# Gate matmuls of a hybrid decoder layer: two heads stacked over 128 rows, or one head on each half of the array

## The chip, the core and the metric

The kernel runs on one core of a Trainium2 chip. The metric is the device time of one execution in microseconds; the time before is the median of 3 runs. TensorE appears in the profile as PE (matmuls) and PEld (weight loads), VectorE as DVE, ScalarE as ACT, GpSimd as POOL, SyncE (which issues most of the DMAs) as SP.

## The reference, cut to what matters

A sequence of 2048 positions with 1024 features is normalised, projected to six groups of 1024 columns, mixed by a short gated convolution (group A) and by a gated linear recurrence (group B, "LRU"), normalised head by head, gated, and projected back. The change touches only the two gates of the LRU, r and i. There are 16 heads of 64 channels; each head has its own 64 by 64 map for r and another for i:

```python
u = causal_depthwise_conv(x_in, conv_w) + conv_b
uh = u.reshape(bsz, s, N_LRU_HEADS, LRU_HEAD_DIM)          # 16 heads of 64
r = jax.nn.sigmoid(jnp.einsum('bshd,hde->bshe', uh, w_a).reshape(bsz, s, d) + b_a)
i = jax.nn.sigmoid(jnp.einsum('bshd,hde->bshe', uh, w_i).reshape(bsz, s, d) + b_i)
a = jnp.exp(RG_LRU_C * r * jax.nn.log_sigmoid(lam))
drive = jnp.sqrt(1 - a * a) * (i * u)                       # h_t = a_t h_{t-1} + drive_t
```

## The kernel before, in words

All large products run on TensorE in the type fp32r. To keep float32 accuracy each operand is split into a high part (a cast to fp32r, on ACT) and a low part (operand minus high part, on DVE or POOL), and a product is made of three matmuls: high by high, high by low, low by high. The products of the big projections are further saved by a seven-product (Strassen-like) scheme on 2 by 2 blocks: `steps` lists 48 + 16 block steps, each of seven products into PSUM banks of 128 by 512 (`mm`, line 886, twelve matmuls for a product: four blocks of the contraction by three parts).

The order of the work is written out by hand. PE goes through the steps; each step has 7 or 8 slots, a slot is one product of 12 matmuls. At each slot's start `tick()` releases what was put into the list `due` by `at(slots, f)`: the elementwise work on ACT, DVE and POOL, and a few extra matmuls. Every engine executes its instructions strictly in the order in which the slots emit them; only semaphores join the engines. Since the releases stand ahead of the slot's product, extra matmuls on PE stand between two products.

Each third step of the first 48 is an LRU step (`lru`, called for h = 0, 1 (halves of the sequence) and k = 0 to 7 (tiles of 128 channels, two heads each)): 16 LRU steps in all. After its column block has come out of PSUM, the following stands at fixed slots: the convolution u (slots 1 to 3); `sth`, the high part of u (slot 5, line 651, ACT); `stl`, the low part (slot 6, through `tt`, line 160, DVE); `gates(0)` at slot 8 and `gates(1)` at slot 10 (line 666, PE), one for each half of the 1024 positions; `sigs(0)` at slot 9 and `sigs(1)` at slot 11 (line 673, four sigmoids of 64 by 512 each, ACT); then the recurrence.

A head has 64 channels, so its map would fill only 64 of the array's 128 rows. Before, the kernel fills the other 64 with the low part. For head j the tile st[j] (128 by 1024) holds the high part of the head's u on one half of the partitions and the low part on the other, and the weights of the head are stored twice, one copy on each half of the partitions. So one matmul over 128 rows gives weight by (high + low); two matmuls, with the weights' high part `bh` and low part `bl`, give the head's r and i for 512 positions. `gates(i)` is 2 heads by 2 matmuls. Each head has its own PSUM tile ("gate" in the profile) from the pool `pss`, which has two buffers; so `gates(1)` can write head j's tile only once `sigs(0)` has read it.

The price of the layout is that high and low parts are made over 64 partitions at a time: `sth` is two casts of 64 by 1024 and `stl` two subtractions of 64 by 1024. `load_gate_w` (lines 608 to 618) fetches the doubled weights by a DMA on SP (line 612) and splits them on POOL (lines 615 and 616) into `bh` and `bl` of 128 by 256.

Other matmuls that lie between products are the head norms' sums (`head_sums`, line 559): four matmuls with weights of 128 by 64. The copies out of a product's PSUM bank are `q` (line 1220), `u` (line 1223), `rr` (line 1226) and `combine` (line 729) on ACT; they share ACT's order with the gates' sigmoids.

Of the kernel before, what the change touches and what calls it, by code (L numbers as in the profile page):

```python
# [12 lines left out]
F32 = mybir.dt.float32  # L13
F32R = mybir.dt.float32r
AF = mybir.ActivationFunctionType
ALU = mybir.AluOpType

P = 128
D = 1024
S = 2048  # L20
C = 512
NC = S // C
NB = C // P
KT = D // P
# [14 lines left out]
def hymba_kernel(ctx: ExitStack, tc: tile.TileContext, x, xt, w_in, par, lamc, w_gate, w_out, final_g, out):  # L39
    nc = tc.nc  # L40
# [6 lines left out]
    small = ctx.enter_context(tc.tile_pool(name="small", bufs=1))  # L47
    psu = ctx.enter_context(tc.tile_pool(name="psu", bufs=5, space=bass.MemoryType.PSUM))
    pss = ctx.enter_context(tc.tile_pool(name="pss", bufs=2, space=bass.MemoryType.PSUM))
# [12 lines left out]
    def wt(tag, name, n=2 * C, dt=F32, bufs=1):  # L62
        return work.tile([P, n], dt, tag=tag, bufs=bufs, name=name)
# [6 lines left out]
    def aux(name):  # L70
        return small.tile([P, C], F32, tag="aux", bufs=4, name=name)
# [69 lines left out]
    def at(slots, *fs):  # L141
        if slots == 0:
            for f in fs:
                f()
        else:
            due.append([slots, fs])
# [12 lines left out]
    def tt(out, a, b, op, eng=None):  # L159
        (eng or nc.vector).tensor_tensor(out=out, in0=a, in1=b, op=op)  # L160
# [176 lines left out]
    def hl_tile(name, n=1):  # L337
        hlc[0] += n
        return [wt("hl", name, dt=F32R, bufs=HL) for _ in range(n)]

    def hl_done(n):
        hlc[0] -= n
# [223 lines left out]
    def finish(d0, h, kt, y, sil, gain, col, row):  # L566
        v = {}

        def f1():
            nc.vector.scalar_tensor_tensor(out=sil, in0=y, scalar=gain, in1=sil,  # L570
                                           op0=ALU.mult, op1=ALU.mult)

        def store():
            for i in range(2):
                nc.sync.dma_start(yd[2 * h + i][:, :, kt, :].rearrange("b p t -> p b t"),
                                  sil[:, i * C:(i + 1) * C].rearrange("p (b t) -> p b t", b=NB))

        def f2():
            nc.scalar.activation(out=y, in_=y, func=AF.Square)
            v["qh"], = hl_tile("qh")  # L580
            nc.scalar.copy(v["qh"], y)

        def f3():
            v["ql"], = hl_tile("ql")
            tt(v["ql"], y, v["qh"].bitcast(F32), ALU.subtract)

        at(d0, f1)
        at(d0 + (1 if kt == KT and h == 0 else 2), store)
        at(d0 + 2, f2)
        at(d0 + 3, f3)  # L590
        at(d0 + 6, lambda: head_sums(h, v["qh"], v["ql"], col, row))
        at(d0 + 7, lambda: hl_done(2))

    def silu(g, late=0):
        sg = [None]

        def f1():
            sg[0] = wt("ig", "sg", bufs=IG)
            nc.scalar.activation(out=sg[0], in_=g, func=AF.Sigmoid)  # L599

        at(2 + late, f1)
        at(4 + late, lambda: tt(g, g, sg[0], ALU.mult, nc.gpsimd))
# [3 lines left out]


    def load_gate_w(k):
        bd = aux("bd")[:, 0:2 * P].rearrange("p (h m) -> p h m", h=2)
        bh = small.tile([P, 2, P], F32R, tag="bh", name="bh")  # L610
        bl = small.tile([P, 2, P], F32R, tag="bl", name="bl")
        nc.sync.dma_start(bd, w_gate[k])

        def part():
            nc.gpsimd.tensor_scalar(out=bh, in0=bd, scalar1=1.0, scalar2=0.0, op0=ALU.mult, op1=ALU.add)
            nc.gpsimd.tensor_tensor(out=bl, in0=bd, in1=bh.bitcast(F32), op=ALU.subtract)

        at(3, part)
        return bh, bl

    LO, HI = slice(0, 64), slice(64, P)
    N2 = 2 * C

    def lru(h, k, late=0):
        o1 = wt("o1", "xl", n=N2 + 4)
        g = wt("o2", "gl", bufs=O2)
        if h == 0:
            nc.gpsimd.memset(o1[:, 0:4], 0.0)
        else:
            nc.scalar.copy(o1[:, 0:4], hx[:, k, :])  # L630
        v = {}
        lw = [pt[:, LW + 8 * j + k:LW + 8 * j + k + 1] for j in range(4)]

        def c0():
            v["u"] = wt("u", "u")
            nc.scalar.activation(out=v["u"], in_=o1[:, 1:1 + N2], func=AF.Identity, scale=lw[0],  # L636
                                 bias=pt[:, LB + k:LB + k + 1])

        def cj(j):
            nc.vector.scalar_tensor_tensor(out=v["u"], in0=o1[:, 1 + j:1 + j + N2], scalar=lw[j],  # L640
                                           in1=v["u"], op0=ALU.mult, op1=ALU.add)

        def keep():
            if h == 0:
                nc.scalar.copy(hx[:, k, :], o1[:, N2:N2 + 4])

        def sth():
            v["st"] = st = hl_tile("st", 2)
            at(6, lambda: hl_done(2))
            for j, hi in enumerate((LO, HI)):  # L650
                nc.scalar.copy(st[j][hi], v["u"][hi])

        def stl():
            st = v["st"]
            for j, (hi, lo) in enumerate(((LO, HI), (HI, LO))):
                tt(st[j][lo], v["u"][hi], st[j][hi].bitcast(F32), ALU.subtract)

        def gates(i):
            sl = slice(i * C, (i + 1) * C)
            if i == 0:  # L660
                v["r"], v["i"] = wt("r", "r"), wt("ig", "i", bufs=IG)
            v["ps"] = ps = []
            for j in range(2):
                ps.append(pss.tile([P, C], F32, tag="s", name="gate"))
                for n in range(2):
                    nc.tensor.matmul(ps[j], v["gw"][n][:, j, :], v["st"][j][:, sl],  # L666
                                     start=(n == 0), stop=(n == 1))

        def sigs(i):
            sl = slice(i * C, (i + 1) * C)  # L670
            for j, (hi, lo) in enumerate(((LO, HI), (HI, LO))):
                for g_, src, bias in ((v["r"], hi, BA), (v["i"], lo, BI)):
                    nc.scalar.activation(out=g_[hi, sl], in_=v["ps"][j][src], func=AF.Sigmoid,  # L673
                                         bias=pt[src, bias + k:bias + k + 1])


        def s0():
            tt(v["u"], v["i"], v["u"], ALU.mult)

        def s1():  # L680
            v["T"] = wt("ig", "T", bufs=IG)
            nc.scalar.activation(out=v["T"], in_=v["r"], func=AF.Tanh, scale=nklam[:, k:k + 1])

        def s1b():
            nc.scalar.activation(out=v["r"], in_=v["r"], func=AF.Exp, scale=klam[:, k:k + 1])

        def s2():
            nc.scalar.activation(out=v["T"], in_=v["T"], func=AF.Sqrt)

        def s3():  # L690
            nc.vector.scalar_tensor_tensor(out=v["u"], in0=v["r"], scalar=1.0, in1=v["u"],
                                           op0=ALU.add, op1=ALU.mult)

        def s4():
            tt(v["u"], v["T"], v["u"], ALU.mult)

        def s5():
            r = v["r"]
            init = 0.0 if h == 0 else hl[:, k:k + 1]
            nc.vector.tensor_tensor_scan(out=r, data0=r, data1=v["u"], initial=init,  # L700
                                         op0=ALU.mult, op1=ALU.add)
            if h == 0:
                nc.vector.tensor_copy(hl[:, k:k + 1], r[:, N2 - 1:N2])

        def out_():
            finish(0, h, KT + k, v["r"], g, pt[:, LG + k:LG + k + 1], 2 * R, KT + k)

        def gw():
            v["gw"] = load_gate_w(k)

        def put(which, bank, other):
            dst = {11: o1[:, 4:4 + C], 12: o1[:, 4 + C:4 + N2], 21: g[:, 0:C], 22: g[:, C:N2]}[which]
            combine(dst, bank, other)
            if which == 12:
                at(1, c0)
                at(2, lambda: cj(1), lambda: cj(2), keep, gw)
                at(3, lambda: cj(3))
                for slots, *fs in ((5, sth), (6, stl), (8, lambda: gates(0)), (9, lambda: sigs(0)),
                                   (10, lambda: gates(1)), (11, lambda: sigs(1)), (12, s1, s0),
                                   (13, s1b), (14, s2, s3), (15, s4), (16, s5), (17, out_)):  # L720
                    at(slots + late, *fs)
            if which == 21:
                silu(g, late)

        return put

    def combine(dst, bank, other):
        if other is None:
            nc.scalar.copy(dst, bank)
        else:  # L730
            tt(dst, bank, other, ALU.add)
# [188 lines left out]
    with tc.manual_schedule(engines={ENG.PE, ENG.Activation, ENG.DVE, ENG.Pool, ENG.SP}):  # L920
# [176 lines left out]
        for n in range(PLAIN, N):  # L1097
            kind, h, k = steps[n]
# [185 lines left out]
```

## Time and profile before

| | |
|---|---|
| time, median of 3 runs | 1418.91 us (1418.45 to 1420.51) |
| profiled execution, first to last instruction | 1418.1 us, 0.8 us under that median |
| mean granted TensorE clock | 0.981 |
| PE busy | 1336.5 us, 5732 matmuls |
| DVE busy | 1069.9 us |
| ACT busy | 782.6 us |
| POOL busy | 242.6 us |

A row of the timeline gives the start in us, the length, the engine, the line, the operation, output<-inputs, the shape, the count, and in brackets the idle time of the engine before it with what ended it. A matmul's length runs from its issue to its modelled end, so consecutive matmuls overlap: what a matmul costs the stream is the distance from its start to the next one's start. A row of the groups gives the count, then busy us and mean ns of one, then the engine's idle time before them.

### The profile page before, as it was taken

To read this page: it belongs to the slowest core of one execution; us is meant where nothing else is said; L and a number is where in the kernel's file an instruction comes from. 1 tells how busy PE (TensorE), PEld (TensorE's weight loads), DVE (VectorE), ACT (ScalarE), POOL (GpSimd) and SP (SyncE) were. 2 spreads that over 40 slices of the span, in tenths; PEclk is the share of its full clock that TensorE was granted. 3 is DMA by queue.
4 is the path that set the end of the run, shared out by engine and by line. 5 is a ranking of instruction groups with operands and counts; after the bars stand their busy time and mean duration, and the time that the engine had idled before them with its cause. 6 is when DMAs were issued, how large, how long until landed. Compare 5 with 4: busy or idle time off the path is not lost.

```text
span 1418.1 us, 16977 instructions
## 1 busy us (share of the span) xinstructions
PE 1336.5 (94%) x5732; PEld 1072.3 (76%) x5732; DVE 1069.9 (75%) x1273; ACT 782.6 (55%) x1165; POOL 242.6 (17%) x159
## 2 busy tenths in 40 slices
PE   6989999999999997899998999998996999988997
PEld 5867777778777775677886878786874888867886
DVE  6778788898989989777767667665667647657885
ACT  7485757666566666375563645463656323343443
POOL 2104333433534430101000000101010000000000
PEclk9999999999999998999999999999997999999999
DMA  5147797898888865730899999998979998697643
GB/s 213 30 141 256 274 280 212 310 326 284 310 280 293 315 242 198 240 97 30 291 315 339 331 339 333 368 294 302 300 259 340 352 304 260 223 390 284 214 155 144
DMA packets 165191, 371.02 MB, mean 262 GB/s; under 512 B 17265, under 2 KB 52465, under 8 KB 165105
## 3 DMA queue, kind: packets, MB, share of 16 engines
q1 hardware_dynamic: 164816, 369.63, 76.3%
q8 instruction: 45, 0.74, 0.2%
q14 instruction: 42, 0.34, 0.1%
q10 hardware_dynamic: 288, 0.32, 0.1%
HBM read 224.45 MB, written 145.43 MB: 261 GB/s over the span
## 4 chain that ended last, share of the span: by engine, by line
PE 65%; DMA 13%; ACT 9%; DVE 8%; issue 3%; SPq 2%; POOL 0%; DVEq 0%; ACTq 0%; POOLq 0%
PE bank L886 60%; PE norm_ps L559 2%; DMA sd<-s 2%; ACT i L673 2%; ACT r L673 2%; PE gate L666 2%; DMA s<-so 2%; DVE s L160 2%; DVE tl L160 1%; DMA yd<-gl 1%; DMA zr<-rsd 1%; DVE traw L160 1%; DMA raw<-in_w_in_dram 1%; DMA traw<-in_w_out_dram 1%; DMA raw<-yd 1%
## 5 line engine op out<-in xcount | busy, mean ns | idle before, releaser
L886 PE MATMUL bank<-th,s 128*128 128x512 f32 x3608 | 1147.0, 395 | 41.5 <-DMA s<-so 9.8
L886 PEld LDWEIGHTS bank<-th,s 128*128 128x128 f32 x3608 | 685.3, 190 | 204.4 <-ACT u L1223 12.2
L886 PE MATMUL bank<-tl,s 128*128 128x512 f32 x1804 | 710.5, 394 | 6.3 <-DVE tl L160 6.0
L886 PEld LDWEIGHTS bank<-tl,s 128*128 128x128 f32 x1804 | 342.9, 190 | 81.4 <-DVE tl L160 10.4
L160 POOL TENSOR_TENSOR s<-raw,s 128x512 fp32r<-128x512 f32 x62 | 118.9, 1931 | 256.4 <-ACT s L197 180.2
L197 ACT CAST s<-raw 128x512 fp32r<-128x512 f32 x136 | 81.8, 616 | 59.6 <-PE bank L886 43.4
L1223 ACT COPY u<-bank 128x512 f32<-128x512 f32 x58 | 34.0, 587 | 141.3 <-PE bank L886 90.9
L160 DVE TENSOR_TENSOR s<-s,s 128x512 fp32r<-128x512 f32 x102 | 103.5, 1015 | 5.4 <-ACT s L197 5.4
L160 DVE TENSOR_TENSOR tl<-traw,th 128x512 fp32r<-128x512 f32 x102 | 70.0, 711 | 47.5 <-ACT th L454 29.1
L160 POOL TENSOR_TENSOR gb<-gb,sg 128x1024 f32<-128x1024 f32 x16 | 41.8, 2611 | 351.4 <-ACT sg L599 331.4
L160 DVE TENSOR_TENSOR s<-raw,s 128x512 fp32r<-128x512 f32 (+1 forms) x120 | 89.8, 771 | 9.9 <-ACT s L197 5.3
L1220 ACT COPY q<-bank 128x512 f32<-128x512 f32 x58 | 33.8, 583 | 79.2 <-PE bank L886 74.2
L160 DVE TENSOR_TENSOR raw<-raw,zr 128x512 f32<-128x512 f32 x64 | 49.6, 801 | 29.6 <-DMA zr<-rsd 29.6
L197 ACT CAST s<-s 128x512 fp32r<-128x512 f32 x102 | 62.8, 616 | 5.9 <-DVE s L160 5.9
L640 DVE SCALAR_TENSOR_TENSOR u<-xl,pt,u 128x1024 f32<-128x1024 f32 x48 | 64.5, 1344 | 0.8 <-ACT u L636 0.2
L1226 ACT COPY rr<-bank 128x512 f32<-128x512 f32 x58 | 33.9, 584 | 47.8 <-PE bank L886 47.7
L160 DVE TENSOR_TENSOR st<-u,st 64x1024 fp32r<-64x1024 f32 x32 | 52.0, 1626 | 1.0
L750 DVE SCALAR_TENSOR_TENSOR t<-p,pt,t 128x1024 f32<-128x1024 f32 x32 | 47.6, 1486 | 4.9 <-ACT t L747 4.1
L160 POOL TENSOR_TENSOR gl<-gl,sg 128x1024 f32<-128x1024 f32 x16 | 45.8, 2862 | 20.1 <-ACT sg L599 20.1
L160 DVE TENSOR_TENSOR ob<-bank,rr 128x512 f32<-128x512 f32 x18 | 12.2, 689 | 48.0 <-ACT rr L1226 48.0
L636 ACT ACTIVATE u<-xl,pt 128x1024 f32<-128x1024 f32 x16 | 19.9, 1245 | 46.8 <-DVE xl L160 46.8
L673 ACT ACTIVATE r<-gate,pt 64x512 f32<-64x512 f32 x64 | 43.8, 684 | 2.4 <-PE gate L666 1.8
(162 smaller groups left out, 1355.9 us busy)
## 6 DMA issues: line engine op xcount, KB each, us to landing
sd<-s SPq DMA_DIRECT2D x147, 512.0 KB, 4.8
s<-sd SPq DMA_DIRECT2D x147, 512.0 KB, 5.9
raw<-in_w_in_dram SPq DMA_DIRECT2D x108, 256.0 KB, 5.0
so<-so SPq DMA_DIRECT2D x42, 512.0 KB, 6.0
s<-so SPq DMA_DIRECT2D x42, 512.0 KB, 7.5
raw<-yd SPq DMA_DIRECT2D x64, 256.0 KB, 5.4
traw<-in_w_out_dram SPq DMA_DIRECT2D x56, 256.0 KB, 5.9
yd<-gl SPq DMA_DIRECT2D x32, 256.0 KB, 3.6
```

What stands on the lines that cost most here:

```text
L160: (eng or nc.vector).tensor_tensor(out=out, in0=a, in1=b, op=op)
L197: nc.scalar.copy(dst[i][0], val(i))
L559: nc.tensor.matmul(norm_ps[0], sel[:, s0:s0 + R], q[:, i * C:(i + 1) * C], start=norm_ps[1] == 0, stop=norm_ps[1] == 8 * KT - 1)
L636: nc.scalar.activation(out=v["u"], in_=o1[:, 1:1 + N2], func=AF.Identity, scale=lw[0], bias=pt[:, LB + k:LB + k + 1])
L640: nc.vector.scalar_tensor_tensor(out=v["u"], in0=o1[:, 1 + j:1 + j + N2], scalar=lw[j], in1=v["u"], op0=ALU.mult, op1=ALU.add)
L666: nc.tensor.matmul(ps[j], v["gw"][n][:, j, :], v["st"][j][:, sl], start=(n == 0), stop=(n == 1))
L673: nc.scalar.activation(out=g_[hi, sl], in_=v["ps"][j][src], func=AF.Sigmoid, bias=pt[src, bias + k:bias + k + 1])
L750: nc.vector.scalar_tensor_tensor(out=tcur["t"], in0=p[:, 2 + j:2 + j + N2], scalar=cw[j], in1=tcur["t"], op0=ALU.mult, op1=ALU.add)
L886: nc.tensor.matmul(bank, a[:, js], b, start=start and n == 0, stop=stop and n == 2, skip_group_check=more)
L1220: nc.scalar.copy(q1, bk["A"])
L1223: nc.scalar.copy(u2, bk["A"])
L1226: nc.scalar.copy(rr, bk["A"])
```

## The change

The two heads keep their natural places: head 0 on partitions 0 to 63, head 1 on partitions 64 to 127. `st[0]` is the high part of the whole u, `st[1]` the low part, each made by one instruction over 128 partitions. The weights are stored once (128 by 128). A gate product is now a matmul over 64 rows, `LO` or `HI`, and since high and low no longer lie one above the other, three matmuls are needed for each head: bh by high, bh by low, bl by high (low by low is left out). The matmuls of the two heads alternate, each into its own PSUM tile. `gates(i)` is 6 matmuls of 64 rows where it was 4 of 128.

```diff
     def load_gate_w(k):
-        bd = aux("bd")[:, 0:2 * P].rearrange("p (h m) -> p h m", h=2)
-        bh = small.tile([P, 2, P], F32R, tag="bh", name="bh")
-        bl = small.tile([P, 2, P], F32R, tag="bl", name="bl")
+        bd = aux("bd")[:, 0:P]
+        bh = small.tile([P, P], F32R, tag="bh", name="bh")
+        bl = small.tile([P, P], F32R, tag="bl", name="bl")
...
         def sth():
             v["st"] = st = hl_tile("st", 2)
             at(6, lambda: hl_done(2))
-            for j, hi in enumerate((LO, HI)):
-                nc.scalar.copy(st[j][hi], v["u"][hi])
+            nc.scalar.copy(st[0], v["u"])
 
         def stl():
             st = v["st"]
-            for j, (hi, lo) in enumerate(((LO, HI), (HI, LO))):
-                tt(st[j][lo], v["u"][hi], st[j][hi].bitcast(F32), ALU.subtract)
+            tt(st[1], v["u"], st[0].bitcast(F32), ALU.subtract)
...
-            v["ps"] = ps = []
-            for j in range(2):
-                ps.append(pss.tile([P, C], F32, tag="s", name="gate"))
-                for n in range(2):
-                    nc.tensor.matmul(ps[j], v["gw"][n][:, j, :], v["st"][j][:, sl],
-                                     start=(n == 0), stop=(n == 1))
+            v["ps"] = ps = [pss.tile([P, C], F32, tag="s", name="gate") for _ in range(2)]
+            for n, (w, q) in enumerate(((0, 0), (0, 1), (1, 0))):
+                for j, rows in enumerate((LO, HI)):
+                    nc.tensor.matmul(ps[j], v["gw"][w][rows, :], v["st"][q][rows, sl],
+                                     start=(n == 0), stop=(n == 2))
...
-    gate = np.concatenate([gate, gate], axis=1)
...
-        "w_gate": gate.reshape(KT, 2, P, P).transpose(0, 2, 1, 3),
+        "w_gate": gate.reshape(KT, P, P),
```

What this does to the order, at three places. First, PE at `gates(0)` of the LRU step h = 0, k = 4 (at 329.42 us of the profile), before; gate_2933 and gate_2936 are the PSUM tiles of the two heads, st_2856 and st_2857 the stacked tiles of the two heads:

```order
L886 MATMUL bank_2755<-th_560,s_2753 128x512
L666 MATMUL gate_2933<-st_2856,bh_2779 128x512
L666 MATMUL gate_2933<-st_2856,bl_2780 128x512
L666 MATMUL gate_2936<-st_2857,bh_2779 128x512
L666 MATMUL gate_2936<-st_2857,bl_2780 128x512
L886 MATMUL bank_2943<-th_296,s_2810 128x512
```

The same place in the changed kernel; gate_2939 and gate_2940 are the two heads' tiles, st_2864 the high part and st_2865 the low part of both heads:

```order
L883 MATMUL bank_2763<-th_560,s_2761 128x512
L663 MATMUL gate_2939<-st_2864,bh_2787 128x512
L663 MATMUL gate_2940<-st_2864,bh_2787 128x512
L663 MATMUL gate_2939<-st_2865,bh_2787 128x512
L663 MATMUL gate_2940<-st_2865,bh_2787 128x512
L663 MATMUL gate_2939<-st_2864,bl_2788 128x512
L663 MATMUL gate_2940<-st_2864,bl_2788 128x512
L883 MATMUL bank_2951<-th_296,s_2818 128x512
```

The second head's first matmul stood third of four and stands second of six; `gates(1)` is changed in the same way. Second, ACT around `sth` of the very first LRU step (71.67 us), before:

```order
L729 COPY p<-bank 128x512
L1020 CAST th<-traw 128x512
L651 CAST st<-u 64x1024 x2
L1020 CAST th<-traw 128x512
L935 CAST s<-raw 128x512
L729 COPY xx<-bank 128x512
```

and in the changed kernel:

```order
L726 COPY p<-bank 128x512
L1017 CAST th<-traw 128x512
L650 CAST st<-u 128x1024
L1017 CAST th<-traw 128x512
L932 CAST s<-raw 128x512
L726 COPY xx<-bank 128x512
```

One instruction stands where two stood, and its neighbours keep their order. Third, DVE at `stl` of the same step, before:

```order
L160 TENSOR_TENSOR tl<-traw,th 128x512
L160 TENSOR_TENSOR t_787<-traw 128x512
L160 TENSOR_TENSOR s<-raw,s 128x512
L160 TENSOR_TENSOR p<-p,xx 128x512
L160 TENSOR_TENSOR st<-u,st 64x1024 x2
L750 SCALAR_TENSOR_TENSOR t<-p,pt,t 128x1024 x2
```

and in the changed kernel:

```order
L160 TENSOR_TENSOR tl<-traw,th 128x512
L160 TENSOR_TENSOR t_786<-traw 128x512
L160 TENSOR_TENSOR s<-raw,s 128x512
L160 TENSOR_TENSOR p<-p,xx 128x512
L160 TENSOR_TENSOR st<-u,st 128x1024
L747 SCALAR_TENSOR_TENSOR t<-p,pt,t 128x1024 x2
```

Again one instruction for two. On SP and POOL nothing changes place: the DMA of line 612 and the two POOL instructions keep their order at half the size.

## The prediction, made before the result was known

> **What bounds the kernel now.** I read the page first, for the engines' shares:
>
> ```profile
> span 1418.1 us, 16977 instructions
> PE 1336.5 (94%) x5732; PEld 1072.3 (76%) x5732; DVE 1069.9 (75%) x1273; ACT 782.6 (55%) x1165; POOL 242.6 (17%) x159
> ```
>
> PE is busy for 94% of the span: time is won where PE's stream gets shorter or where PE waits. So next comes the list of PE's waits. Three of its rows bear on the change:
>
> ```profile
> PE bank L886 <- ACT u L1223: 8.8, 8, 4.2
> PE bank L886 <- ACT rr L1226: 3.1, 5, 1.4
> PE gate L666 <- ACT i L673: 3.8, 16, 0.7
> ```
>
> (total us, times, longest.) The last is the gates' own wait. Then the timeline, at one LRU step of the steady part, PE:
>
> ```profile
> 325.49 0.39 PE L886 MATMUL bank<-th,s 128*128 128x512 f32 x1
> 325.72 0.40 PE L559 MATMUL norm_ps<-qh,sel 128*64 128x512 f32 x1
> ...
> 326.42 0.40 PE L559 MATMUL norm_ps<-ql,sel 128*64 128x512 f32 x1
> 326.65 0.39 PE L886 MATMUL bank<-th,s 128*128 128x512 f32 x1
> ...
> 329.42 0.40 PE L666 MATMUL gate<-st,bh 128*128 128x512 f32 x1
> ...
> 330.35 0.40 PE L886 MATMUL bank<-th,s 128*128 128x512 f32 x1
> ...
> 335.83 0.40 PE L666 MATMUL gate<-st,bh 128*128 128x512 f32 x1
> 336.07 0.40 PE L666 MATMUL gate<-st,bl 128*128 128x512 f32 x1
> 336.64 0.50 PE L666 MATMUL gate<-st,bh 128*128 128x512 f32 x1 [0.17 <-ACT i L673]
> 336.97 0.39 PE L666 MATMUL gate<-st,bl 128*128 128x512 f32 x1
> 337.20 0.40 PE L886 MATMUL bank<-th,s 128*128 128x512 f32 x1
> ```
>
> and ACT's side of the same stretch:
>
> ```profile
> 333.31 0.59 ACT L1220 COPY q<-bank 128x512 f32<-128x512 f32 x1 [2.06 <-PE bank L886]
> 333.79 0.69 ACT L673 ACTIVATE r<-gate,pt 64x512 f32<-64x512 f32 x1
> ...
> 335.90 0.68 ACT L673 ACTIVATE i<-gate,pt 64x512 f32<-64x512 f32 x1
> ```
>
> Two things are to be seen. The first four gate matmuls cost PE 330.35 - 329.42 = 0.93 us, 0.23 each, with no wait. The second four cost more: the second head's first matmul waits until the fourth sigmoid has ended (335.90 + 0.68 = 336.58), since it overwrites what that sigmoid reads. The sigmoids stand on ACT behind the copy q, which itself waits for PE to finish the product that begins at 330.35. So the release at 336.64 stands 6.29 us after the end of the first gate group whatever PE does in between: it moves with PE and cannot be outrun.
>
> **The change, part by part.** The sum is made against the profiled execution (span 1418.1 us) and 0.8 us is added, by which the median of the runs, 1418.9, lies above it.
>
> *High and low parts over 128 partitions.*
>
> ```profile
> L651 ACT CAST st<-u 64x1024 fp32r<-64x1024 f32 x32 | 33.4, 1044 | 1.6 <-DMA so<-so 1.3
> L581 ACT CAST qh<-r 128x1024 fp32r<-128x1024 f32 x16 | 16.8, 1049 | 0.5
> L160 DVE TENSOR_TENSOR st<-u,st 64x1024 fp32r<-64x1024 f32 x32 | 52.0, 1626 | 1.0
> L160 DVE TENSOR_TENSOR ql<-r,qh 128x1024 fp32r<-128x1024 f32 x16 | 20.0, 1251 | 0.0
> ```
>
> A cast over 128 partitions (1049 ns) lasts no longer than one over 64 (1044). So 32 casts become 16 and ACT loses 33.4 - 16.8 = 16.6 us. The subtractions go from 52.0 us to about 16 x 1.25 = 20.0, so DVE loses 32 us. On the path this is worth almost nothing:
>
> ```profile
> 325.82 3.46 DVE L160 TENSOR_TENSOR st<-u,st 64x1024 fp32r<-64x1024 f32 x2
> 336.04 0.69 DVE L160 TENSOR_TENSOR xx<-bank,u 128x512 f32<-128x512 f32 x1 [2.31 <-PE bank L886]
> ```
>
> After the subtractions DVE runs out of work and stands idle for 2.31 us until PE closes a bank; ACT stands idle for 2.06 us ahead of the copy q. What the two engines save in front of these waits makes the waits longer. I cost it at nothing in 15 of the 16 LRU steps.
>
> *The first LRU step* is the exception, for there PE waits on just this work:
>
> ```profile
> 72.42 0.39 PE L886 MATMUL bank<-th,s 128*128 128x512 f32 x1
> 78.35 0.77 PE L666 MATMUL gate<-st,bh 128*128 128x512 f32 x1 [5.54 <-ACT hp L755]
> 80.59 0.63 PE L886 MATMUL bank<-th,s 128*128 128x512 f32 x1
> ...
> 71.67 2.11 ACT L651 CAST st<-u 64x1024 fp32r<-64x1024 f32 x2
> 73.81 0.62 ACT L1020 CAST th<-traw 128x512 fp32r<-128x512 f32 x1
> ...
> 74.46 0.69 DVE L160 TENSOR_TENSOR tl<-traw,th 128x512 fp32r<-128x512 f32 x1 [1.36 <-ACT th L1020]
> 76.98 2.47 DVE L160 TENSOR_TENSOR st<-u,st 64x1024 fp32r<-64x1024 f32 x2
> ...
> 60.00:100.00 40.00, 34.40 (x142) 27.53 (x141) 31.56 (x43) 28.86 (x44) 2.64 (x2) 0.91 0.22 77
> ```
>
> The wait is put down to ACT's hp, but the gates need st, and DVE's first subtraction ends at about 76.98 + 2.47/2 = 78.2. One cast less on ACT lets the cast at 73.81 come 1.05 us earlier; DVE, which waited 1.36 us for it, comes 1.05 earlier with all that follows. The clock granted in these 40 us is 0.91, and the four gate matmuls here take 80.59 - 78.35 = 2.24 us; three such shares are 1.68, so 0.56 less. That is -1.6 us. Earlier work falls into the stretch of low clock and may give up to half of it back (-0.8); a shorter gap may also shorten that stretch (at most -3). I take -1.4.
>
> *The gate matmuls.* 16 steps x 2 groups x 6 matmuls of 64 rows replace 16 x 2 x 4 of 128 rows. No row of the profile shows a 64-row matmul. The bounds for a pair, one matmul on the upper and one on the lower rows: if both run at once, one slot of 0.23 us, as any matmul of 512 columns here, the one with half the weight columns (norm_ps) included; if one after the other, two slots, 0.46. Loading does not forbid the lower one:
>
> ```profile
> 39.12 1.03 PE L491 MATMUL tp<-ident,x 128*128 128x128 f32 x8
> 39.91 0.48 PE L886 MATMUL bank<-th,s 128*128 128x512 f32 x1
> ```
>
> Eight matmuls with a weight load of 128 columns each pass in 0.79 us, 0.10 each, so two loads (0.20) fit into a slot of 0.23. I take 0.23, since the two heads share no row of the array, no partition and no PSUM bank, and a slot's length follows the 512 streamed columns; that the halves run at once is an assumption, and the higher end is a rival below. The Trainium skill ("TensorE: Matmul & The Clock Gate", Part 3) says that matmuls on different row groups run concurrently and start within about 4 ns of each other; by that page a pair is one slot too. No run here shows it yet.
>
> First groups: three pairs, 0.70 us, for 0.93, so -0.23 each, 15 x -0.23 = -3.5. Second groups: now one matmul instead of two stands ahead of the wait, and five instead of two behind it. Behind the release stood 0.33 + 0.23 = 0.56 us up to the next product (336.64 to 337.20). Now the second head's first matmul goes out with the first head's second (0.33, as the step after a wait), then a pair (0.23), then the last one (0.23): 0.79. That is +0.23, 15 x 0.23 = +3.5. **The two cancel:** the matmul that is saved is spent again behind the wait. Without the extra 0.10 after the wait it would be +0.12 each, or +1.8; so the two together lie between -1.7 and 0. I take 0, because the 0.33 stands in the row. What is queued behind the wait is only the product at 337.20, which is in the sum; the sigmoids of the second group follow on ACT at 340.70, three us later, and do not feel it:
>
> ```profile
> 340.70 0.69 ACT L673 ACTIVATE r<-gate,pt 64x512 f32<-64x512 f32 x1
> 320.24 1.06 POOL L616 TENSOR_TENSOR bl<-bd,bh 128x256 fp32r<-128x256 f32 x1
> ```
>
> *Changing between 128 and 64 rows*, 64 times. The nearest rows are the head norms, which change between weights of 128 and of 64 columns: 325.49 to 325.72 going in and 326.42 to 326.65 coming out are 0.23 each, as inside a product. So 0 to 0.01 us each; I take +0.3 in all. The Trainium skill ("TensorEngine Tiling (Array Packing)", Key Properties) says that changing the tiling mode drains TensorE. For the change of columns this trace disagrees (0.23, no drain); for rows no run here shows it, so it is a rival.
>
> *Weights*: SP's 16 DMAs of line 612 and POOL's 32 splits are halved in size and keep their places. POOL has finished bl at 321.30, eight us ahead of the gates at 329.42: nothing.
>
> Sum: -1.4 + 0 + 0.3 = -1.1, so 1418.9 - 1.1 = **1417.8 us**. With the ends, -4.7 to +1, it is 1414 to 1420. A difference below 0.2% (2.8 us) is about what a measurement of this kernel can tell from no change, so this is "the same".
>
> **The rivals.**
>
> *Serial halves (slower).* The change does not do what it says: the two halves run one after the other. The first group takes 6 x 0.23 = 1.40 for 0.93, +0.47; behind the release stand 0.33 + 4 x 0.23 = 1.26 for 0.56, +0.70. 15 x 1.17 = +17.5, less about 0.5 in the first step: 1436 us. For it: no pair of overlapping streams is in the trace. Against it: nothing is shared. A pair of length p costs 15 x (5p - 1.16) against now, so with the -1.1 it is measurably slower from p = 0.28 on, well before 0.46.
>
> *A drain at each change of rows (slower).* If the next matmul starts only at its predecessor's end, that is 0.40 - 0.23 = 0.17 us, and 0.27 with the extra 0.10 after a wait. One of the four changes in a step is covered by the gates' wait; 48 x 0.17 to 0.27 is +8 to +13, in all +7 to +12: 1426 to 1431 us. A pair at 0.33, its loads uncovered, lands near the same place. For it speaks the page named above; against it the 0.23 around the head norms.
>
> *Relief of DVE and ACT reaches PE (faster).* PE's waits for the copies u and rr, 8.8 + 3.1 us, would shrink if DVE and ACT came to them earlier. Without the longest u wait (4.2), which lies in another stage, 7.7 us is the most: 1410 to 1416 us. For it: 49 us of work vanish from two engines. Against it: the idle 2.31 and 2.06 us that lie between that work and those waits.
>
> **How the numbers follow.** My case has 0.48, serial halves 0.20, a drain or dear pairs 0.17, relief or a larger gain in the first step 0.15. The forecast is that of the first, whose own range is 1414 to 1420. With the drain and the relief it reaches from 1411 to 1431, which leaves out the serial case. Faster takes the relief and the lower end of my case, 0.15 + 0.08 = 0.23; slower takes both slower rivals, 0.37; the same has 0.40.
>
> **What would show it.** In the changed profile: gate matmuls in pairs that start almost together, a first group of about 0.70 us, a second with a longer wait and about 0.79 us behind it; one cast of 1.05 and one subtraction of 1.25 us in each LRU step, with longer idle times behind them; a first gate group near 77.3 instead of 78.35; 0.23 into and out of the groups. Groups of 1.4 us would mean serial halves, a first matmul that is 0.2 us late at each group's edge a drain, and shorter waits for u and rr the relief. Wrong altogether would be a second group that no longer waits for the sigmoids, for my cancellation rests on that wait.

## The result, and the profile after

| | median, us | runs |
|---|---|---|
| before | 1418.68 | 4, from 1417.56 to 1420.51 |
| changed | 1429.16 | 4, from 1424.09 to 1429.76 |

The ratio is 1.0058, with a 95% interval of 1.0038 to 1.0078: the changed kernel is slower, where no change was forecast (1417.8 us). In a second set of six runs of the changed kernel (told below) the median was 1423.33. The mean of all ten is 1425.2 us, 6.5 above the 1418.68 of before. The profiled execution is the 1424.09.

First the engines' shares, from the page of the changed kernel:

```profile
span 1422.3 us, 17051 instructions
PE 1342.6 (94%) x5796; PEld 1063.1 (75%) x5796; DVE 1042.4 (73%) x1257; ACT 763.3 (54%) x1149; POOL 234.1 (16%) x159
```

DVE has lost 27.5 us of work and ACT 19.3 (32 and 16.6 were foretold), and the span is longer all the same. The groups of the changed kernel show one cast of 1.04 us, as foretold, and one subtraction of 1.56 us in the mean, where 1.25 was foretold, for each LRU step:

```profile
L160 DVE TENSOR_TENSOR st<-u,st 128x1024 fp32r<-128x1024 f32 x16 | 24.9, 1559 | 0.0
L650 ACT CAST st<-u 128x1024 fp32r<-128x1024 f32 x16 | 16.7, 1041 | 0.0
```

The engines behind it got longer idle times, not earlier ends. This is ACT and then DVE in the timeline, at the same LRU step as in the prediction; the brackets were 2.06 and 2.31 before:

```profile
332.25 0.59 ACT L1217 COPY q<-bank 128x512 f32<-128x512 f32 x1 [2.75 <-PE bank L883]
334.83 0.68 ACT L670 ACTIVATE i<-gate,pt 64x512 f32<-64x512 f32 x1
```

```profile
334.97 0.69 DVE L160 TENSOR_TENSOR xx<-bank,u 128x512 f32<-128x512 f32 x1 [3.94 <-PE bank L883]
```

So the loss lies on PE. The list of its waits shows the gates' wait for the sigmoids still there, sixteen times (3.8 us in all before, 4.7 now), and a smaller total for the copies u (8.8 before, 5.9 now; that one is looked at below):

```profile
PE bank L883 <- ACT u L1220: 5.9, 8, 1.4
PE gate L663 <- ACT i L670: 4.7, 16, 0.9
```

Now PE's timeline around the two gate groups of that step. A group is measured here from the start of the last product matmul ahead of it to the start of the second product matmul behind it, so that both its edges are in. In the kernel before the first group is six plain slots, 1.40 us: the four of the prediction's rows (0.93) and one of 0.23 at each edge. These are its two edges:

```profile
329.19 0.39 PE L886 MATMUL bank<-th,s 128*128 128x512 f32 x1
...
330.59 0.39 PE L886 MATMUL bank<-tl,s 128*128 128x512 f32 x1
```

The same stretch of the changed kernel, and behind it the second group:

```profile
327.96 0.39 PE L883 MATMUL bank<-th,s 128*128 128x512 f32 x1
328.28 0.74 PE L663 MATMUL gate<-st,bh 64*128 64x512 f32 x4
328.85 0.40 PE L663 MATMUL gate<-st,bl 64*128 64x512 f32 x2
329.18 0.50 PE L883 MATMUL bank<-th,s 128*128 128x512 f32 x1
329.52 0.40 PE L883 MATMUL bank<-tl,s 128*128 128x512 f32 x1
...
334.54 0.39 PE L883 MATMUL bank<-th,s 128*128 128x512 f32 x1
334.86 0.49 PE L663 MATMUL gate<-st,bh 64*128 64x512 f32 x1
335.56 0.50 PE L663 MATMUL gate<-st,bh 64*128 64x512 f32 x2 [0.21 <-ACT i L670]
...
336.46 0.50 PE L883 MATMUL bank<-th,s 128*128 128x512 f32 x1
336.79 0.39 PE L883 MATMUL bank<-tl,s 128*128 128x512 f32 x1
```

The six matmuls of the first group are issued as three pairs. In the single records, which these rows merge, the two members of a pair start 4 to 10 ns apart (3 to 13 ns over all first groups behind the first step). From 328.28 to 328.85 are two pairs in 0.57 us: the second pair starts 0.33 behind the first, and the third 0.23 behind the second. That much is one slot for a pair, as assumed. What was not foretold lies at the edges: 0.32 from the last product matmul to the first pair where 0.23 is plain; 0.33 from the first pair to the second; 0.33 from the last pair to the product; and 0.34 from the product's first matmul to its second. That is about 0.10 too much four times, two at each change between 128 and 64 rows: 0.2 us for a change, 0.39 for the group (0.09 + 0.10 + 0.10 + 0.10). The group takes 1.55 us where before it took 1.40 and 1.17 was foretold.

The weight loads differ at the same places. In the kernel before, the load of a gate's weights begins in the preceding matmul's slot (its matmul starts at 329.42):

```profile
329.20 0.19 PEld L666 LDWEIGHTS gate<-st,bh 128*128 128x128 f32 x1
```

In the changed kernel, at both edges, nothing is loaded ahead:

```profile
327.74 0.19 PEld L883 LDWEIGHTS bank<-th,s 128*128 128x128 f32 x1
328.28 0.30 PEld L663 LDWEIGHTS gate<-st,bh 64*128 64x128 f32 x4 [0.35 <-issue]
...
329.18 0.19 PEld L883 LDWEIGHTS bank<-th,s 128*128 128x128 f32 x1 [0.37 <-issue]
```

The load for the first pair begins at 328.28, with its matmul and not a slot ahead of it, after 0.35 us in which no load ran; so does the load for the first product matmul behind the group, after 0.37. The bracket says "issue": the profile shows nothing that is waited for. The prediction's rows have the same 0.33 once without a change of rows: from 336.64 to 336.97, behind the wait for the sigmoid, where the load (at 336.63) also began with its matmul. So the 0.10 ahead of the second matmul goes with a load that did not run ahead. What the 0.09 ahead of the first one goes with, the records do not show.

The first LRU step got shorter. In PE's timeline there, the wait is now for DVE's subtraction:

```profile
71.75 0.39 PE L883 MATMUL bank<-th,s 128*128 128x512 f32 x1
72.07 0.50 PE L663 MATMUL gate<-st,bh 64*128 64x512 f32 x2
76.43 0.50 PE L663 MATMUL gate<-st,bh 64*128 64x512 f32 x2 [3.86 <-DVE st L160]
...
77.09 0.63 PE L883 MATMUL bank<-th,s 128*128 128x512 f32 x1
```

From the last product matmul ahead to the first behind it is 77.09 - 71.75 = 5.34 us, where before it was 80.59 - 72.42 = 8.17: 2.8 less.

One pair of the gates now stands ahead of this wait (72.07), since it needs only the high part.

**The sum from the trace.** A steady first group loses 0.16 (1.55 for 1.40). A steady second group loses 0.43 (336.79 - 334.54 = 2.25, where before it was 1.83: from 335.83 to 337.20 by the prediction's rows, and a slot of 0.23 at each edge). 15 steps at 0.59 would be +8.9. Two groups are not steady: the first group at 138.8 us took 1.74 before, and the second group at 606.0, where the wait for the sigmoids is longer, went from 3.28 to 4.55. With each of the 15 steps at its own figure the first groups give +2.0 and the second groups +7.1. The first step gives -2.8, and +0.2 in its second group. Together that is +6.5 us.

Is anything else at work? From the second group of the first step to that of the eighth (86.91 to 523.39 us before, 84.03 to 524.12 now) PE loses 3.61 us, and the groups in this stretch account for 3.48. There the sum closes. Behind 590 us it is less clean: 1.8 us more are lost up to the last gates, and behind the last gates, where the change places nothing, the stretch is 4.1 us shorter than before (356.7 for 360.8). That need not come from the new layout: in the kernel before with another edit (told below) the same stretch is 3.0 shorter too (357.8). The 1.8 is not explained. So the spans differ by 4.2. The profiled execution's time is 5.4 above the median before, and the mean of the ten runs 6.5.

### The profile page after: what moved, and what is told of

It reads as the page before. It is cut to its first block, busy times and chain, and to the rows that moved or that the text cites. A ratio compares the mean times of both kernels' runs of the same rounds, so it can differ in the third digit from the quotient of the medians.

```text
span 1422.3 us, 17051 instructions
## 1 busy us (share of the span) xinstructions
PE 1342.6 (94%) x5796; PEld 1063.1 (75%) x5796; DVE 1042.4 (73%) x1257; ACT 763.3 (54%) x1149; POOL 234.1 (16%) x159
## 4 chain that ended last, share of the span: by engine, by line
PE 54%; DMA 12%; DVE 11%; ACT 7%; issue 5%; SPq 2%; POOL 1%; DVEq 0%; ACTq 0%; POOLq 0%
PE bank L883 51%; DMA yd<-gl 2%; DMA zr<-rsd 2%; DVE s L160 2%; PE norm_ps L559 2%; PE gate L663 2%; DMA raw<-yd 2%; ACT i L670 1%; DMA traw<-in_w_out_dram 1%; DMA sd<-s 1%; ACT r L670 1%; DVE r L697 1%; DVE tl L160 1%; DVE traw L160 1%; DMA so<-so 1%
## 5 line engine op out<-in xcount | busy, mean ns | idle before, releaser
L160 DVE TENSOR_TENSOR s<-s,s 128x512 fp32r<-128x512 f32 x102 | 100.0, 981 | 5.4 <-ACT s L197 5.4
L160 DVE TENSOR_TENSOR s<-raw,s 128x512 fp32r<-128x512 f32 (+1 forms) x120 | 96.3, 825 | 9.7 <-ACT s L197 5.3
L160 DVE TENSOR_TENSOR xx<-bank,u 128x512 f32<-128x512 f32 x15 | 10.4, 690 | 55.3 <-PE bank L883 55.3
```

## The experiments

The first theory is that the loss is the price of changing between 128 and 64 rows. Its rivals: a pair of 64-row matmuls costs more than a slot, whatever stands next to it; or the longer second group, with its wait, is to blame. The seven kernels were measured in two series, the first four below and the last three, each with the kernel before beside it (medians 1418.72 and 1418.81). The changed kernel itself, with its second set of runs (1423.33), was in the second series. A second question was how much of the time hangs on the gates' wait for the sigmoids, on which the prediction's cancellation rests.

**Six matmuls over all 128 rows** (in the changed kernel; each head's weights are padded with zeros on the other head's rows):

```diff
-                for j, rows in enumerate((LO, HI)):
-                    nc.tensor.matmul(ps[j], v["gw"][w][rows, :], v["st"][q][rows, sl],
+                for j in range(2):
+                    nc.tensor.matmul(ps[j], v["gw"][w][:, j, :], v["st"][q][:, sl],
```

> The changed kernel with its gate matmuls over all 128 rows: the weights of each head are padded with zeros on the other head's rows, so the same six matmuls need no change of rows. If the changes of rows cost about 0.39 us per group (0.09 and 0.10 going in, the same coming out), these extras are gone here and a first group is six plain slots: from the last product matmul ahead of it to the second one behind it 1.40 + 2 x 0.23 = 1.86 us (before 1.40, changed 1.55), a second group 1.83 + 3 x 0.23 = about 2.5 us; in all 15 x (0.31 + 0.28) = 9 us more than the changed kernel. If the extras come from the order of the six matmuls or from their waits, they stay, and the groups are 0.39 us longer still: 2.25 and 2.9 us, 21 us more than the changed kernel.

Measured: 1432.49 us, ratio to before 1.0098 (1.0083 to 1.0113). PE's timeline:

```profile
330.46 0.39 PE L883 MATMUL bank<-th,s 128*128 128x512 f32 x1
330.69 1.10 PE L663 MATMUL gate<-st,bh 128*128 128x512 f32 x4
331.62 0.63 PE L663 MATMUL gate<-st,bl 128*128 128x512 f32 x2
332.09 0.39 PE L883 MATMUL bank<-th,s 128*128 128x512 f32 x1
332.32 0.40 PE L883 MATMUL bank<-tl,s 128*128 128x512 f32 x1
```

The group is eight slots of 0.23 (1.86 us), with no extra anywhere: 0.23 in, 0.23 out. The instructions, their order and PSUM tiles are those of the changed kernel; only the rows are not halved. So the extra 0.39 comes with the halved rows, and not with six matmuls, their order or their waits. The kernel is 9.2 us slower than the changed one's second set, where 9 was expected. This run takes the pairs away together with the changes; a run below adds changes and keeps the pairs. Against the 0.39 the pairs save three slots (0.70): with halves, a group of six is 0.31 cheaper than without.

**The sigmoids of the first group one slot earlier**, on the changed kernel and on the kernel before. ACT then runs them ahead of the copy q, and the second group's PSUM tiles are free in time:

```diff
-(8, lambda: gates(0)), (9, lambda: sigs(0)),
+(8, lambda: gates(0), lambda: sigs(0)),
```

> The changed kernel with the first half's four sigmoids given to ACT right behind the first gate group (slot 8) and ahead of the copy q, not one slot later. If the wait of the second group is set by those sigmoids standing behind q, it is gone: the second group costs what the first does (1.55 us instead of 2.25), 15 x 0.70 = 10.5 us less than the changed kernel. If the wait is only moved (q comes later on ACT, and PE then waits for a bank), nothing is gained.

> The kernel before with the same move of the four sigmoids. If the wait for them is worth what the rows show (second group 1.83 us against 1.40 for the first), this is 15 x 0.43 = 6.5 us faster than before, about 1412 us. If the wait only moves to a bank, it is the same as before.

Measured: the changed kernel with this edit 1410.99 us, ratio 0.9948 (0.9932 to 0.9963); the kernel before with this edit 1408.83, ratio 0.9931 (0.9916 to 0.9946). ACT's timeline in the first, with the last of the four sigmoids, then the copy q:

```profile
330.88 0.68 ACT L670 ACTIVATE i<-gate,pt 64x512 f32<-64x512 f32 x1
...
332.12 0.58 ACT L1217 COPY q<-bank 128x512 f32<-128x512 f32 x1
```

and PE's timeline of its second group:

```profile
334.05 0.39 PE L883 MATMUL bank<-th,s 128*128 128x512 f32 x1
334.36 0.73 PE L663 MATMUL gate<-st,bh 64*128 64x512 f32 x4
...
335.26 0.50 PE L883 MATMUL bank<-th,s 128*128 128x512 f32 x1
335.60 0.40 PE L883 MATMUL bank<-tl,s 128*128 128x512 f32 x1
```

The last sigmoid ends at 330.88 + 0.68 = 331.56, ahead of q, where in the changed kernel it ends at 335.51, behind q. The wait is gone, and the second group costs 1.55 us, the same as the first. The extras at the edges are all there still (0.31 in, 0.34 behind). In the kernel before with this edit PE's second group is six plain slots (1.40):

```profile
334.22 0.39 PE L886 MATMUL bank<-th,s 128*128 128x512 f32 x1
...
335.61 0.39 PE L886 MATMUL bank<-tl,s 128*128 128x512 f32 x1
```

Added over all 15 later steps, the second groups get 12.1 us shorter in the changed kernel (against its second profile) and 8.1 in the kernel before. Steady groups alone would give 15 x (2.25 - 1.55) = 10.5 and 15 x (1.83 - 1.40) = 6.5; the rest is the group near 606 us, whose longer wait is gone too. Measured, the gains are 12.3 (against the second set of the changed kernel) and 9.9. The first is accounted for. In the kernel before 1.8 us are left over, and they are not shown to come from the gates: PE's total wait for the copies u falls from 8.8 to 6.4,

```profile
PE bank L886 <- ACT u L1223: 6.4, 8, 1.9
```

but the seven waits for u up to 490 us are the same one by one, to 0.02 us. What shrank is a single wait behind the last gates (4.24 us at 1283.9, here 1.88 at 1274.9), and in the changed kernel, where no sigmoid was moved, it is 1.36.

Without the wait in either kernel the change still costs 2.2 us (1410.99 for 1408.83). In the two traces the 31 groups behind the first add up to +4.6, and the first group gives 2.2 back: 2.4. The kernel before with this edit is the fastest of all that ran, faster than both original kernels.

**High and low parts over 64 partitions again**, in the changed kernel:

```diff
-            nc.scalar.copy(st[0], v["u"])
+            for rows in (LO, HI):
+                nc.scalar.copy(st[0][rows], v["u"][rows])
...
-            tt(st[1], v["u"], st[0].bitcast(F32), ALU.subtract)
+            for rows in (LO, HI):
+                tt(st[1][rows], v["u"][rows], st[0][rows].bitcast(F32), ALU.subtract)
```

> The changed kernel with high and low parts made in two instructions of 64 partitions each, as before, on the new layout; the matmuls stay as changed. If the savings of ACT and DVE reach PE in the first LRU step alone, this is 1 to 3.5 us slower than the changed kernel, all of it ahead of 90 us. If the savings also shortened PE's waits for u and rr, it is up to 7 us slower, spread over the steps.

Measured: 1425.59 us, ratio to before 1.0049 (1.0033 to 1.0066). That is 2.3 above the median of the changed kernel's second set, 3.6 below that of its first, and inside the range of its ten runs; by the times alone the two can't be told apart. The trace can tell: the groups of the steady part are the same (1.55 and 2.25), and the difference is in the first LRU step, here in PE's timeline:

```profile
72.00 0.39 PE L885 MATMUL bank<-th,s 128*128 128x512 f32 x1
...
77.34 0.79 PE L665 MATMUL gate<-st,bh 64*128 64x512 f32 x1 [3.81 <-DVE st L160]
...
79.75 0.79 PE L885 MATMUL bank<-th,s 128*128 128x512 f32 x1
```

79.75 - 72.00 = 7.75 us from product to product, where the changed kernel has 5.34 in its first profile and 5.83 in its second (and the kernel before 8.17). So the relief of ACT and DVE is worth 1.9 to 2.4 us, in the step in which PE waits for that work. Only 0.7 of it is an earlier end of the wait (77.34 - 72.00 = 5.34 for 76.43 - 71.75 = 4.68); the rest lies behind the wait, where the matmuls are longer here: the granted clock from 60 to 100 us is 0.87, where both profiles of the changed kernel have 0.96. Elsewhere the relief doesn't reach PE. PE's total wait for the copies u is 6.0 us in this kernel and 5.9 in the changed one, so the fall from 8.8 is not the relief's; it is the single wait at 1283.9 us again.

**The changed kernel once more**, beside the two that follow:

> The changed kernel once more, beside the other runs of this call. The group costs in its trace (1.55 and 2.25 us against 1.40 and 1.83 before) give 15 x (0.16 + 0.43) = +8.8 us less about 3 in the first step, so about +6 against before; its first runs had +10 and their profile +4. If the groups and the first step are all there is, it comes out near 1425; if the rest of the program also gets longer (waits for DMAs), near 1429, and the profile shows where.

Measured: 1423.33 us (1421.45 to 1424.98, six runs), ratio to before 1.0033 (1.0021 to 1.0044). The interval overlaps that of the first four runs, whose median was 1429.16. The trace holds an execution of 1421.45 us with the same steady groups (1.55 and 2.25), and its groups add up to +6.3 against before. Single runs lie between 1421 and 1425 or near 1429, and that does not go by set: the four runs of the last experiment below do both within one series (1423.24 and 1423.54, 1428.66 and 1428.85). Where the executions near 1429 spend the other five us isn't shown, since no profile of one exists.

**One more change of rows**: a matmul over 128 rows, whose weights are zeros, behind the first pair of each group of the changed kernel. It adds a slot and two changes of rows:

```diff
+                if n == 0:
+                    nc.tensor.matmul(ps[0][:R], sel[:, 0:R], v["st"][0][:, sl],
+                                     start=False, stop=False)
```

> The changed kernel with one more matmul in each gate group, behind the first pair: all 128 rows, 64 weight columns that are zero, added to the first head's sum. So the rows change twice more in each group. If each change of rows costs about 0.2 us, a first group grows by a slot and two changes, 0.23 + 0.39, from 1.55 to about 2.17 us, and the kernel by 30 x 0.62 = 18 us (less what the second group's wait hides, at most 15 x 0.5). If the extra belongs to a group once (its first matmul, its waits), it grows by the slot alone, to 1.78 us, and the kernel by 7 us.

Measured: 1443.34 us, ratio to before 1.0176 (1.0161 to 1.0191), 20.0 above the changed kernel beside it. PE's timeline of a first group:

```profile
332.68 0.39 PE L886 MATMUL bank<-th,s 128*128 128x512 f32 x1
...
333.42 0.44 PE L666 MATMUL gate<-st,sel 128*64 128x512 f32 x1
...
334.45 0.50 PE L886 MATMUL bank<-th,s 128*128 128x512 f32 x1
334.78 0.40 PE L886 MATMUL bank<-tl,s 128*128 128x512 f32 x1
```

The group takes 334.78 - 332.68 = 2.10 us, 0.55 more than 1.55. The slot is 0.23 of it, so two more changes cost 0.32, 0.16 each. (The added matmul has 64 weight columns; by the prediction's rows of the head norms that costs nothing.) The pairs are as before, so a pair that is dear in itself would not show this. The second group went from 2.25 to 2.83. 15 x (0.55 + 0.58) = 17 of the 20 us are in the groups.

**The three matmuls of head 0 first, then those of head 1**, in the changed kernel:

```diff
-            for n, (w, q) in enumerate(((0, 0), (0, 1), (1, 0))):
-                for j, rows in enumerate((LO, HI)):
+            for j, rows in enumerate((LO, HI)):
+                for n, (w, q) in enumerate(((0, 0), (0, 1), (1, 0))):
```

> The changed kernel with the three matmuls of the first head ahead of the three of the second. If matmuls start in the order in which they stand, only the first head's third and the second head's first run at once: five slots for three, a first group of 1.55 + 0.46 = 2.0 us; a second group stays at 2.25, since three matmuls still stand behind the wait. In all 15 x 0.46 = 7 us slower than the changed kernel. If each half of the array takes its own matmuls as they come, the first group stays at 1.55 and the time is the changed kernel's.

Measured: 1426.1 us (1423.24 to 1428.85), ratio to before 1.0059 (1.004 to 1.0079); it can't be told from the changed kernel's ten runs. PE's timeline:

```profile
329.12 0.39 PE L883 MATMUL bank<-th,s 128*128 128x512 f32 x1
329.43 0.74 PE L663 MATMUL gate<-st,bh 64*128 64x512 f32 x4
330.00 0.40 PE L663 MATMUL gate<-st,bl 64*128 64x512 f32 x2
330.33 0.50 PE L883 MATMUL bank<-th,s 128*128 128x512 f32 x1
330.67 0.40 PE L883 MATMUL bank<-tl,s 128*128 128x512 f32 x1
```

If matmuls started in the order of the program, only the last of head 0 and the first of head 1 could run side by side: five slots and 2.0 us. The group took 1.55 us as before, and the records show four matmuls with bh and then two with bl, though the program has bh, bh, bl of head 0 ahead of bh, bh, bl of head 1. That the program's order is by head is seen in the second group, where head 1 waits for the sigmoid and head 0's three go first:

```profile
336.01 0.73 PE L663 MATMUL gate<-st,bh 64*128 64x512 f32 x2
336.58 0.39 PE L663 MATMUL gate<-st,bl 64*128 64x512 f32 x1
336.73 0.73 PE L663 MATMUL gate<-st,bh 64*128 64x512 f32 x2
```

So here each half of the rows took its own matmuls in its own order, and the order between the heads did not matter. Of the two outcomes named before the run the second came out; for PE's matmuls on two halves it also sets right the statement, made ahead of the prediction, that every engine executes strictly in order. The theory of the change of rows isn't touched by it.

## Why the prediction was wrong, step by step

- **Relief of ACT and DVE, nothing in 15 steps**: held. The idle times ahead of q and xx grew from 2.06 and 2.31 to 2.75 and 3.94 us, and undoing the relief alone left the steady groups and the waits for u as they were. DVE's saving was put too high (32 us for 27.5), which cost nothing, as it is off the path.
- **The first LRU step, -1.4 us**: inside its ends (-0.8 to -3), but too small: -2.8, and -2.3 in the second profile. The wait ended 1.25 us earlier (4.68 behind the product, where it was 78.35 - 72.42 = 5.93), about the 1.05 foretold. The gate matmuls behind it took 0.66 us (76.43 to 77.09), where 1.68 was reckoned: one pair runs ahead of the wait, which the prediction did not see. And the price of low clock that was set against it did not come; in the stretch from 60 to 100 us the granted clock (third number from the end) was 0.96 where before it was 0.91, by the view of the windows:

```profile
60.00:100.00 40.00, 35.28 (x150) 27.45 (x148) 32.29 (x44) 29.44 (x45) 2.63 (x2) 0.96 0.29 103
```

- **A pair is one slot of 0.23 us**: held; the pair's members start 3 to 13 ns apart and the second and third pairs are 0.23 apart. The rival of serial halves is out. The Trainium skill ("TensorE: Matmul & The Clock Gate", Part 3) puts that distance at about 4 ns, and the trace agrees (4 ns is the median). The same section says that matmuls start strictly in program order; the run with the heads one after the other differs (1.55 us, four bh ahead of two bl), and there the measurement decides.
- **The wait moves with PE and cannot be outrun; one slot saved ahead is spent behind it**: held. From the product behind the first group to the release are 335.56 - 329.18 = 6.38 us, where before it was 6.29. The 0.09 is the late second matmul of that product (329.52 - 329.18 = 0.34 for 0.23), which the first group's 1.55 already holds. Behind the release stand 0.90 us up to the next product; 0.79 was foretold, and the 0.11 is the change of rows.
- **Changing between 128 and 64 rows, 0 to 0.01 us each, +0.3 in all**: this is the step that failed. It was priced by the head norms' rows, which change the weight columns and not the rows, and there 0.23 showed no extra. A change of rows costs about 0.2 us here (0.39 for in and out; 0.16 each in the run with one more). In the first group both changes are paid: -0.23 foretold, +0.39, so +0.16. In the second, the change on the way in (334.54 to 334.86) hides in the wait for the sigmoid, and the change on the way out shows in full, 0.11 ahead of the product and 0.10 ahead of its second matmul: +0.23 foretold, +0.20, so +0.43. The term is 15 x (0.39 + 0.20) = +8.9 in steady steps, instead of +0.3.

The rival that named this, a drain at each change of rows, had +8 to +13 for it and 1426 to 1431 us in all. Its count was right: one of the four changes in a step is covered by the wait. The term of +8.9 lies inside; of the measured medians 1429.2 lies inside and 1423.3 below. Its working was that the next matmul starts only at its predecessor's end. The records show something nearer to two parts: 0.09 until the first matmul, and 0.10 until the second, which goes with a load that did not run ahead. The Trainium skill ("TensorEngine Tiling (Array Packing)", Key Properties) says that a change of the tiling mode drains TensorE. A cost of about 0.2 us at each change of rows fits that; that PE empties in between is not shown, for the ends of matmuls are modelled, and only starts are measured. The head norms' 0.23 tells nothing against it for rows, and no row here shows whether 64 weight columns are a change of the mode at all.

Left open are the five us between the executions below 1425 and those near 1429. The groups account for +6.5, about 1425.

## What to carry to other kernels

Packing two 64-row matmuls into one slot is real, but a group of them pays about 0.4 us of its own where it stands between 128-row matmuls, nearly two slots. By these figures (an estimate) it wins where it saves two slots or more in one uninterrupted group: against six full matmuls it saves three and gained 0.31, and against the four of before it saved one and lost 0.16. Don't price a change of rows by a change of columns that looks like it in the profile; if the trace does not show an operation, let the rival that names its cost set the forecast until a row speaks against just that. A wait that moves with PE is better removed than fed with shorter work: moving four sigmoids ahead of one copy gained 9.9 us in the kernel before, of which its trace shows 8.1 in the gates.

## What the runs showed of the hardware that was not expected

- A change between matmuls over 128 and over 64 rows cost 0.16 to 0.20 us, in the steady groups about half of it ahead of the first matmul and half ahead of the second; with the rows kept at 128 and the same six matmuls there was no such cost (0.23 in and out).
- No weights were loaded ahead across such a change: PEld stood idle for 0.35 and 0.37 us and began with the matmul, where in the kernel before a load begins some 0.22 us ahead of its matmul.
- Matmuls on the two halves of the rows did not keep the program's order between them: with head 0's three ahead of head 1's, the group took the same 1.55 us, with four bh ahead of two bl.
